# A hybrid encoder block on one core: S5 steps behind the gate copies, keys stacked before queries on another queue, a pool placed lower, and row pairs 64 bytes apart

## The chip, the cores and the metric

The kernel runs on one core of one Trainium2 chip. The metric is the device time of one execution in microseconds (us). The time before is the median of three timed runs, 1764.08 us (1761.85 to 1765.89). One more execution was taken with the hardware profiler; it took 1765.39 us, and its traced span is 1763.6 us.

## The reference, cut to what matters

One layer of an encoder block is applied to two request groups with the same weights: a prompt of 256 tokens and a sample of 512 tokens, 768 token rows in all, of width 1024. Everything is float32.

```python
def layer(x, mem, ...):
    h = rmsnorm(x, norm_mix_g)
    u, q, k, v, qm, gl = split(h @ w_in)              # 1024, 1024, 1024, 1024, 1024, 3072 columns
    z = gelu(s5(u, forward) + s5(u, backward) + d * u)  # 64 groups of 16 channels, 64 complex states
    s5_out = z * sigmoid(z @ s5_w_glu)
    diff_out = diff_attention(q, k, v)                # 8 heads, two softmax maps each, rotary, q/k norms
    mem_out = memory_attention(qm, rmsnorm(mem))      # 4 heads, 256 memory tokens
    br = stack([s5_out, diff_out, mem_out]) @ w_branch   # three 1024 x 1024 products
    merged = sum_n(sigmoid(gl_n + b_gate_n) * br_n)
    x = x + merged @ w_out
    g, up = split(rmsnorm(x) @ w_gate_up)
    return x + (silu(g) * up) @ w_down
```

## The kernel before, in words

**Products.** A float32 product is made of three TensorE products of rounded parts: each operand is split into a high part and a low remainder, and `mm3` (L748) issues high by high, high by low and low by high (L751 to L753). So each matrix of activations lies in SBUF as a pair of tiles: `H` (the normalised rows), `z`, `s5o` (the S5 branch's output), `xd` (differential attention's output), `mgd` (the merged rows), `f` and `dxh`/`dxl` (the FFN's). `pair(pool, name)` makes two tiles in a pool; `s5o` and `mgd` take the place that `H` had, on the right-hand side of SBUF. In nearly all products one operand is a pair of rows and the other a pair of weights, `wh` and `wl`. Names in the profile carry them: `wo<-wh,mgdhi` is a product of the output projection with the high parts of the merged rows.

**Weights.** `WStream` loads half of a weight chunk at a time (512 KB) on SyncE's queue, and splits it ahead of use: `wh` by a ScalarE copy (L595), `wl` by a VectorE subtraction (L601), or, while `by_dma` is set, by a ScalarE copy (L598) and a DMA that adds.

**Order.** The program is written as Python loops over chunks. Other work is woven in by generators that a "pace" advances by a tick per piece. A tile scheduler with a simulated timeline then fixes the order of the instructions on each engine; `tc.issue_after(x)` lets it place the following instructions only behind `x`. A tile's address follows from its pool: pools are stacked from two sides of SBUF, and a pool that is opened over the place of closed ones waits for those tiles' last users.

**The stages on TensorE.** (1) Memory keys, values and queries, and the cross attention, whose output becomes `Xm`. Within it and after it come the u chunks 0 to 3: eight 128-row tiles `ut`, each filled from two products (256 tokens copied by VectorE at L1075, 512 by ScalarE at L1073) and stored by SyncE to `u_scr` (`u_flush`, L282). Before a tile is filled, GpSimd zeroes three of its columns (L277). Chunks 0 and 1 use two buffers. Chunks 2 and 3 run while VectorE derives the S5 parameters, the last of which is `s5bb` (L242); their tiles come in turn from the pool `up` on the right and `up3` on the left. `up3` lies where the S5 work pool `pq` is opened afterwards, and the first tile of `pq` is `G`.

(2) The gates `gl`: 24 tiles of 128 columns, M = 0 to 23, in 12 weight chunks, each tile with a 256-token and a 512-token part that ScalarE copies out as `glt` (L1116). Between them the S5 steps run by ticks. For a group of four, `build` makes `G` on VectorE (L293, L296 to L298) and four small copies `s5bpad` on ScalarE (L310), and `response` multiplies them on TensorE (`psK`, L326). During M = 2 and 3 the ticks are bound behind the gate copy.

(3) Differential attention. Per head, `stack(h, i)` (L1217) transposes queries (i = 0) or keys (i = 1) on TensorE (`qkT`, L1230), makes the high parts on ScalarE (L1236) and the remainders on VectorE (`kl`, L1238; queries L1240); a head's keys are also copied to the other half of the partitions by two DMAs on GpSimd's queue (L1244, `kst<-kst`). The scores `sc` of the head (L1279, L1280) need all of it. In `diff_attend` head 0 is stacked queries first. `finish` (L1332) scales a head's output into `do`, and a DMA on ScalarE's queue stores that to `br_scr` (L1340).

(4) The branch of cross attention (`branch(2)`), woven with the tail of differential attention; at its last chunk `tail` closes attention's pools and opens the pool `XB`, in which the pair `z` is made (`zhi`, L745 on ScalarE, `zlo` on VectorE) for the half-GLU `glu`. `do` was the last tile of the pool `da2`, in the range over which `XB` is placed. Then come branch 0 with `s5o`, branch 1 with `xd`, whose last step writes the pair `mgd`, the output projection `wo` (512 columns of weights move against the rows of `mgd`), and the FFN with its products `gate`, `up` and `dn`.

Of the kernel before, what the change touches and what calls it, by code (L numbers as in the profile page):

```python
# [8 lines left out]
F32 = mybir.dt.float32  # L9
F32R = mybir.dt.float32r  # L10
# [13 lines left out]
class S5:  # L24
# [362 lines left out]
    def states(self, qd):  # L387
# [33 lines left out]

        S, T = new("X", 3), new("T", 1)
        i = slice(1, n - 1)
        vt(S[:, :, i], W[:, :, i], cs[:, i].unsqueeze(1).to_broadcast([128, 2, n - 2]), mul)
        vt(T[:, :, i], W[:, ::-1, i], sn[:, ::-1, i], mul)
        vt(S[:, :, i], S[:, :, i], T[:, :, i], add)
        S = [S[:, c].rearrange("p (g k) -> p g k", g=4)[:, :, 1:98] for c in range(2)]
        st["S"] = S

    def outputs(self, qd, y_scr):  # L430
# [3 lines left out]
        i = slice(1, 98)  # L434
        U, TT, S = st["U"], st["TT"], st["S"]
        G = st["G"]
# [50 lines left out]
TOK = 768  # L487
# [139 lines left out]
def hybrid_block(ctx, tc, A, outs, consts):  # L627
    nc = tc.nc
    v, act, gp, pe = nc.vector, nc.scalar, nc.gpsimd, nc.tensor
# [18 lines left out]
    def uid(s):  # L648
        cnt[0] += 1
        return f"{s}_{cnt[0]}"  # L650
# [167 lines left out]

    hctx, qctx, mctx = ExitStack(), ExitStack(), ExitStack()
    hp_ = hctx.enter_context(tc.tile_pool(name="H", bufs=1, side="right"))  # L820
    H = tuple(hp_.tile([128, 8, TOK], F32R, name=f"H{w}", tag="X" + w) for w in ("hi", "lo"))
    k1 = qctx.enter_context(tc.tile_pool(name="ma1", bufs=1, side="right"))
    mrs = k1.tile([128, 4], F32, name="mrs")
    k2 = qctx.enter_context(tc.tile_pool(name="ma2", bufs=2, side="right"))
# [48 lines left out]
    def mem_q(h):  # L873
# [9 lines left out]
        for sg, (c0, n) in enumerate(SEGS):  # L883
            sq = k3.tile([128, 2, n], F32, name=uid("mqsq"), tag=f"mqsq{sg}")
            sqs.append(sq)
            for m in range(2):
                ps = psd("mq")
                dense_fm(ps, w, m, H, c0, n)
                split_evac(qTh[:, m, c0 : c0 + n], qTl[:, m, c0 : c0 + n], ps[:, 0:n])
# [81 lines left out]
    with tc.tile_pool(name="nrm", bufs=1) as pool, tc.tile_pool(name="nrmg", bufs=1) as pg:  # L971
# [14 lines left out]
        for t0 in (0, 2):  # L986
            for k0 in range(0, 8, 2):
                ps = env.psb("nT")
                pv = ps.rearrange("p (k t) -> p k t", k=2)
                for k in range(2):  # L990
                    for t in range(2):
                        c = 128 * (k0 + k)
# [46 lines left out]
        for tt in range(TILES):  # L1039
            to_features(norm_rows(pool, xr[tt], rs[tt], g), H, tt)  # L1040
            next(units)
# [16 lines left out]
    s5 = S5(nc, tc, env, A, consts)  # L1058
    s5.open_dram(s5ctx)
    uctx = ExitStack()  # L1060
    up = uctx.enter_context(tc.tile_pool(name="utp", bufs=2))

    def u_chunk(c, tick, pools=None):
        w = W.get()
        for m in range(2):
            ut = s5.u_tile(pools[m] if pools else up, 2 * c + m)
            for sg, (c0, n) in enumerate(SEGS):
                ps = psd("u")
                dense_fm(ps, w, m, H, c0, n)
                src = ps[:, 0:n].rearrange("p (k j) -> p j k", j=8)  # L1070
                dst = ut[:, ::-1, 1:33] if sg == 0 else ut[:, ::-1, 34:98]
                if sg:
                    act.activation(dst, src, AF.Copy)  # L1073
                else:
                    v.tensor_copy(dst, src)  # L1075
                tick(1.0 + sg)
            s5.u_flush(ut, 2 * c + m)
# [12 lines left out]
    up = uctx.enter_context(tc.tile_pool(name="utp2", bufs=1, side="right"))  # L1090
    with tc.tile_pool(name="s5gap", bufs=1) as gap, tc.tile_pool(name="s5scr", bufs=1) as scr:

        gap.tile([128, 512], F32, name="s5gap")
        s5.params(scr, env.psb)
        with tc.tile_pool(name="utgap", bufs=1) as gap2, tc.tile_pool(name="utp3", bufs=1) as up3:
            gap2.tile([128, 9372], F32, name="utgap")
            for c in (2, 3):
                u_chunk(c, lambda w: None, (up, up3))
    uctx.close()


    with ExitStack() as c2:
        s5.open_work(c2)
        psum(1, b=4, w=1, d=2)
        glp = c2.enter_context(tc.tile_pool(name="glp", bufs=2))
        pace = Pace(s5.steps(y_scr), S5_RATE)
        for c in range(12):
            W.by_dma = True
            w = W.get()
            for m in range(2):  # L1110
                M = 2 * c + m
                for sg, (c0, n) in enumerate(SEGS):
                    gt = glp.tile([128, 512], F32, name=uid("glt"), tag="glt")
                    ps = psd("gl")
                    dense_fm(ps, w, m, H, c0, n)
                    out = act.activation(gt[:, 0:n], ps[:, 0:n], AF.Identity, bias=bg[:, M : M + 1])  # L1116
                    nc.sync.dma_start(gl_scr[M][:, c0 : c0 + n], gt[:, 0:n])
                    with tc.issue_after(out.ins) if M in (2, 3) else ExitStack():
                        pace.tick(1.0 + sg)
        pace.drain()  # L1120
    psum(2, a=2, b=3, d=3)
# [2 lines left out]

    x1ctx, xbctx, dctx, wctx = (ExitStack() for _ in range(4))
    stg = x1ctx.enter_context(tc.tile_pool(name="stg", bufs=2))
    k1 = dctx.enter_context(tc.tile_pool(name="da1", bufs=1))
    k2 = dctx.enter_context(tc.tile_pool(name="da2", bufs=2))
    q1 = wctx.enter_context(tc.tile_pool(name="dq1", bufs=1))
# [2 lines left out]
    tC = q1.tile([128, 4, 4, 64], F32, name="ropeC")  # L1132
    tS = q1.tile([128, 4, 4, 64], F32, name="ropeS")
    nlam = k1.tile([128, 1], F32, name="nlam")
    k2.tile([128, TOK], F32, name="do_", tag="do", bufs=1)

    rp = q1.tile([128, TILES, 256], F32, name="ropesrc", tag="ropet")
    tab, lv = (rp[:, t].rearrange("p (t c) -> p t c", c=64) for t in range(2))
# [31 lines left out]
    KL = [k1.tile([128, TOK], F32R, name=f"kl{i}") for i in range(4)]  # L1170
    for i, t in enumerate(KL):
        gp.memset(t[64 - 64 * (i % 2) : 128 - 64 * (i % 2)].bitcast(F32), 0.0)
    RO, VV, ST = {}, {}, {}

    def qk_units(h):
        w = W.get()
# [2 lines left out]
        for tt in range(TILES):  # L1179
            ps = psd("qk")  # L1180
            dense_tm(ps, w, 0, 256, H, tt)
            act.activation(r[:, tt], ps[:, 0:256], AF.Copy)
# [34 lines left out]
    def stack(h, i):  # L1217

        ro = RO[h]
        tag = "qk"[i]
        T = [k2.tile([128, TOK], F32R, name=uid(tag + "st"), tag=f"{tag}{m}") for m in range(2)]
        if i:
            kl = KL[2 * (h % 2) : 2 * (h % 2) + 2]
        for t0, t1 in ((0, 2), (2, 6)):
            ps = env.psb("qkT")
            for t in range(t0, t1):
                pe.transpose(ps[:, 128 * (t - t0) : 128 * (t - t0) + 128],  # L1230
                             ro[:, t, 128 * i : 128 * i + 128], env.ident)
            cs = slice(128 * t0, 128 * t1)
            for m in range(2):
                s, o = slice(64 * m, 64 * m + 64), slice(64 - 64 * m, 128 - 64 * m)
                src = ps[s, 0 : 128 * (t1 - t0)]
                act.activation(T[m][s, cs], src, AF.Copy)  # L1236
                if i:
                    v.tensor_tensor(out=kl[m][s, cs], in0=src, in1=T[m][s, cs].bitcast(F32), op=sub)  # L1238
                else:
                    v.tensor_tensor(out=T[m][o, cs], in0=src, in1=T[m][s, cs].bitcast(F32), op=sub)  # L1240
        if i:
            for m in range(2):
                s, o = slice(64 * m, 64 * m + 64), slice(64 - 64 * m, 128 - 64 * m)
                gp.dma_start(T[m][o], T[m][s])  # L1244
            ST[h] = ST[h] + [T, kl]
            RO.pop(h)
        else:
            ST[h] = [T]

    def diff_attend():  # L1250

        while 0 not in RO:
            yield
        stack(0, 0)
        yield
        stack(0, 1)
        for _ in range(2):
            yield
        N = 8 * TILES
        X = {}  # L1260
# [70 lines left out]

        def finish(h):  # L1332
            osb = X.pop(("h", h))[0]
            do = k2.tile([128, TOK], F32, name=uid("do"), tag="do", bufs=1)
            for t0, t1 in ((0, 2), (2, 6)):
                ps = env.psb("oT")
                for t in range(t0, t1):
                    pe.transpose(ps[:, 128 * (t - t0) : 128 * (t - t0) + 128], osb[:, t], env.ident)
                act.activation(do[:, 128 * t0 : 128 * t1], ps[:, 0 : 128 * (t1 - t0)], AF.Copy, scale=subg)
            act.dma_start(br_scr[h], do)  # L1340

        for i in range(N + 5):
            h, tt = divmod(i, TILES)
# [46 lines left out]
    with tc.tile_pool(name="gelu", bufs=1) as yp:  # L1390
        for m in range(2):
            gelu_load(m, yp)
        for j, h in enumerate(DIFF_HEADS):
# [3 lines left out]
            for n_v, u_ in enumerate(v_units(last // 2) if h is None else qk_units(h)):  # L1397
                n_unit += 1
                W.by_dma = n_unit >= LOADED and not final
                m, r = divmod(n_unit, GELU_UNITS)  # L1400
# [4 lines left out]
                if final and n_v % 2:  # L1405

                    t = slice(128 * (n_v - 1), 128 * (n_v + 1))
# [77 lines left out]
    with ExitStack() as c5:  # L1485
        c5.push(hctx)
        XA = hp_
# [5 lines left out]
        def pair(pool, nm):  # L1493
            return tuple(pool.tile([128, 8, TOK], F32R, name=uid(nm + w), tag="X" + w) for w in ("hi", "lo"))

        def branch(n_, X, first=False, MG=None, tick=None, hook=None):
            for c in range(4):
# [76 lines left out]

        branch(2, Xm, first=True, tick=dat.tick, hook=tail)
        x1, XB, Z = L["x1"], L["XB"], L["Z"]
        S = pair(XA, "s5o")
        for c in range(4):
            w = W.get()
            if c == 0:  # L1580
# [6 lines left out]
            for m in range(2):  # L1587
                M = 2 * c + m
                t = gtp.tile([128, TOK], F32, name=uid("gt"), tag="glr")
# [17 lines left out]
                    tc.keep_in_program_order(gp.dma_start(x1[t], xs[t]))  # L1607

        branch(0, S, hook=rows_in)
        MG = pair(XA, "mgd")  # L1610
        branch(1, Xd, MG=MG)
        mgctx.close()
        psum(3, d=5, b=3)
# [37 lines left out]
        for c in range(2):  # L1651
            w = [W.get(False)]
# [203 lines left out]
    with ExitStack() as c7:  # L1856
# [12 lines left out]
        for i, (p, g) in enumerate(ITEMS):  # L1869
# [10 lines left out]
            for t in range(3):  # L1880
                c = slice(128 * t, 128 * t + 128)
# [3 lines left out]
            if g == NG - 1:  # L1885
                r, f, op = HOME[p]
                for t in range(3):
                    o = x1[3 * r + t][:, 512 * f : 512 * f + 512]
# [51 lines left out]
```

## Time and profile before

| | before |
|---|---|
| timed runs, us | 1761.85, 1764.08, 1765.89 (median 1764.08) |
| profiled execution, us | 1765.39 |
| its traced span, us | 1763.6 |
| TensorE busy, us (share of the span) | 1740.1 (99%) |
| VectorE busy | 1267.4 (72%) |
| ScalarE busy | 889.0 (50%) |
| GpSimd busy | 276.0 (16%) |
| mean granted TensorE clock | 0.997 |

TensorE's matmuls are pipelined: a duration of one is longer than the distance from its start to the next one's, so durations are compared with each other and not added. The number in brackets behind a row of the timeline is the idle time of the engine just before it, and what ended it. In the rows of windows the columns are the stretch, its length, the busy time of TensorE, its weight loads, VectorE, ScalarE and GpSimd (with the number of instructions), the granted TensorE clock, the DMA engines' busy share and GB/s.

### The profile page before, as it was taken

What the parts mean: (1) busy time and instruction counts of PE and PEld (TensorE: products, weight loads), DVE (VectorE), ACT (ScalarE), POOL (GpSimd) and SP (SyncE); (2) the same over time, 40 slices, a digit from 0 to 9 for tenths busy, and PEclk for the clock granted to TensorE, in tenths of its full rate; (3) what the DMA queues carried; (4) which work ended last, traced back from release to release, by engine and by line L of the source; (5) the groups of instructions that cost most, each with busy time, mean ns of one, the idle gap of its engine ahead of it and who ended that gap; (6) DMA issues with size and microseconds to landing.
All of it is one profiled execution on the core that took longest, in us unless ns stands there. A gap on an engine that the chain in (4) does not pass through costs nothing.

```text
span 1763.6 us, 29524 instructions
## 1 busy us (share of the span) xinstructions
PE 1740.1 (99%) x11242; PEld 1611.4 (91%) x11242; DVE 1267.4 (72%) x2349; ACT 889.0 (50%) x1856; POOL 276.0 (16%) x296
## 2 busy tenths in 40 slices
PE   9999999999999998999999999999999999999999
PEld 8999988899999998999989888888889999998887
DVE  6755747799999779797877535453598777776775
ACT  6444543786767347777765433232343333334443
POOL 0000000000000101101110002000026555551220
PEclk9999999999999999999999999999999999999999
DMA  7222635755556457345484337331322323238964
GB/s 252 83 90 88 129 118 116 183 130 150 142 158 158 123 137 193 80 107 118 104 196 129 122 115 247 124 104 59 90 76 99 108 90 108 90 108 272 265 142 109
DMA packets 209662, 234.11 MB, mean 133 GB/s; under 512 B 57832, under 2 KB 173296, under 8 KB 209520
## 3 DMA queue, kind: packets, MB, share of 16 engines
q1 hardware_dynamic: 184080, 164.05, 30.8%
q0 software_dynamic: 24288, 65.02, 17.3%
q10 hardware_dynamic: 1152, 3.15, 0.5%
q8 instruction: 89, 1.46, 0.3%
q14 instruction: 53, 0.43, 0.1%
HBM read 165.78 MB, written 41.22 MB: 117 GB/s over the span
## 4 chain that ended last, share of the span: by engine, by line
PE 59%; DMA 2%; issue 1%; DVE 1%; ACT 1%; POOL 0%; SPq 0%; DVEq 0%; ACTq 0%; POOLq 0%
PE br L752 4%; PE br L751 4%; PE br L753 4%; PE gate L751 3%; PE up L751 3%; PE gate L753 3%; PE up L752 3%; PE gate L752 3%; PE up L753 3%; PE dn L752 3%; PE dn L753 3%; PE dn L751 3%; PE av L1316 2%; PE qk L752 2%; PE qk L753 2%; PE qk L751 2%
## 5 line engine op out<-in xcount | busy, mean ns | idle before, releaser
L595 ACT ACTIVATE wh<-wr 128x1024 fp32r<-128x1024 f32 x124 | 140.6, 1134 | 69.1 <-PE br L752 28.3
L601 DVE TENSOR_TENSOR wl<-wr,wh 128x1024 fp32r<-128x1024 f32 x82 | 108.4, 1325 | 83.8 <-ACT wh L595 81.9
L751 PE MATMUL gl<-Hhi,wh 128*128 128x256 f32 (+1 forms) x384 | 132.0, 344 | 0.0
L753 PE MATMUL gl<-Hhi,wl 128*128 128x256 f32 (+1 forms) x384 | 129.1, 336 | 0.0
L752 PE MATMUL gl<-Hlo,wh 128*128 128x256 f32 (+1 forms) x384 | 129.0, 336 | 0.0
L751 PE MATMUL qk<-wh,Hhi 128*128 128x256 f32 x384 | 108.8, 283 | 1.1 <-ACT V L1214 0.7
L752 PE MATMUL qk<-wl,Hhi 128*128 128x256 f32 x384 | 109.1, 284 | 0.0
L599 POOL DMA_DIRECT2D wl<-wr x42 | 36.6, 872 | 459.4 <-ACT wl L598 442.5
L753 PE MATMUL qk<-wh,Hlo 128*128 128x256 f32 x384 | 108.3, 282 | 0.0
L752 PE MATMUL dn<-wld,dxh 128*128 128x512 f32 x231 | 89.6, 389 | 0.0
L751 PE MATMUL dn<-whd,dxh 128*128 128x512 f32 x231 | 89.5, 389 | 0.0
L753 PE MATMUL dn<-whd,dxl 128*128 128x512 f32 x231 | 88.9, 389 | 0.0
L753 PEld LDWEIGHTS gl<-Hhi,wl 128*128 128x128 f32 x384 | 72.2, 188 | 7.9
L752 PEld LDWEIGHTS gl<-Hlo,wh 128*128 128x128 f32 x384 | 72.4, 189 | 7.3
L751 PEld LDWEIGHTS gl<-Hhi,wh 128*128 128x128 f32 x384 | 72.4, 189 | 6.9
L751 PEld LDWEIGHTS qk<-wh,Hhi 128*128 128x128 f32 x384 | 73.1, 190 | 2.2 <-ACT V L1214 0.9
L557 ACT ACTIVATE wh_S<-ws 128x512 fp32r<-128x512 f32 x70 | 41.2, 626 | 65.5 <-PE up L752 35.2
L752 PEld LDWEIGHTS qk<-wl,Hhi 128*128 128x128 f32 x384 | 73.1, 190 | 0.6
L753 PEld LDWEIGHTS qk<-wh,Hlo 128*128 128x128 f32 x384 | 73.3, 191 | 0.3
L1285 DVE TENSOR_REDUCE nm<-sc 128x1 f32<-128x512 f32 (+1 forms) x96 | 56.9, 599 | 22.2 <-PE sc L1280 21.3
L1287 ACT ACTIVATE p<-sc,nm 128x512 f32<-128x512 f32 (+1 forms) x96 | 59.1, 618 | 22.4 <-DVE nm L1285 22.1
L558 DVE TENSOR_TENSOR wl_S<-ws,wh_S 128x512 fp32r<-128x512 f32 x70 | 58.0, 852 | 16.2 <-ACT wh_S L557 16.2
(481 smaller groups left out, 6025.0 us busy)
## 6 DMA issues: line engine op xcount, KB each, us to landing
wr<-in_w_in_dram SPq DMA_DIRECT2D x48, 512.0 KB, 5.0
wr<-in_w_gate_up_dram SPq DMA_DIRECT2D x44, 512.0 KB, 3.6
wl<-wr POOLq DMA_DIRECT2D x42, 512.0 KB, 5.2
wr<-in_w_branch_dram SPq DMA_DIRECT2D x24, 512.0 KB, 4.3
glr<-gl_scr POOLq DMA_DIRECT2D x24, 384.0 KB, 3.4
hid_scr<-fa SPq DMA_DIRECT2D x11, 768.0 KB, 6.4
wr<-in_w_mem_kv_dram SPq DMA_DIRECT2D x16, 512.0 KB, 3.5
wr<-in_w_in_dram SPq DMA_DIRECT2D x32, 256.0 KB, 4.4
```

The lines of the kernel that those rows point to most:

```text
L557: self.nc.scalar.activation(f(hi), src, AF.Copy)
L558: self.nc.vector.tensor_tensor(out=f(lo), in0=src, in1=f(hi).bitcast(F32), op=ALU.subtract)
L595: self.nc.scalar.activation(hi, r, AF.Copy)
L599: self.nc.gpsimd.dma_start(lo, r.bitcast(F32R), accum_op=ALU.add)
L601: self.sub.tensor_tensor(out=lo, in0=r, in1=hi.bitcast(F32), op=ALU.subtract)
L751: pe.matmul(ps, wh, xh, start=start, stop=False, **kw)
L752: pe.matmul(ps, wh, xl, start=False, stop=False, **kw)
L753: pe.matmul(ps, wl, xh, start=False, stop=stop, **kw)
L1285: v.tensor_reduce(out=nm[:, m : m + 1], in_=ps, axis=AX.X, op=ALU.max, negate=True)
L1287: act.activation(pm[:, 0:n], ps, AF.Exp, bias=nm[:, m : m + 1], accum_out=s1s[:, tt : tt + 1] if m == 0 else s2)
L1316: pe.matmul(po[:, 0:128], aT[:, 128 * k : 128 * k + 128], V[:, c0 // 128 + k, 128 * (h % 2) : 128 * (h % 2) + 128], start=(k == 0), stop=( ...
```

## The change: what it does

The change has five parts.

1. `u`: chunks 2 and 3 use one tile (`up`, one buffer, on the right); the second pool `up3` and the filler below it are gone. Each `ut` of these chunks is zeroed after the tile before it has been stored.
2. Gates: the ticks of the S5 steps are bound behind the gate copies for M = 0 to 3, and not only for M = 2 and 3.
3. `do` gets a pool of its own, `dop`, opened below attention's pools, in a range that `XB` does not cover.
4. Head 0 is stacked keys first. The copies of the keys go out on SyncE's queue for heads 0 and 7, and stay on GpSimd's for the others. `ST[h]`, which the scores wait for in the program, is filled when both halves are there.
5. `rows_pair` makes `H`, `s5o` and `mgd`: tiles that are 64 bytes longer, with the high part at the start and the low part 64 bytes in, or, for `mgd`, the other way round. In the addresses as built, taken modulo 256 bytes, the weights `wh` and `wl` are at 160 before and after. `H` and `s5o` were at 224 and 224 (high, low) and are at 96 and 224; `mgd` was at 224 and 224 and is at 160 and 160. `z`, `xd`, `f` and the `dn` operands are at 160 in both.

```diff
-    H = tuple(hp_.tile([128, 8, TOK], F32R, name=f"H{w}", tag="X" + w) for w in ("hi", "lo"))
+    def rows_pair(nm, off=0):
+        ts = (hp_.tile([128, 8 * TOK + 16], F32R, name=nm + w, tag="X" + w) for w in ("hi", "lo"))
+        return tuple(t[:, o : o + 8 * TOK].rearrange("p (k t) -> p k t", k=8) for t, o in zip(ts, (off, 16 - off)))
+
+    H = rows_pair("H")
...
-            ut = s5.u_tile(pools[m] if pools else up, 2 * c + m)
+            ut = s5.u_tile(up, 2 * c + m)
...
-        with tc.tile_pool(name="utgap", bufs=1) as gap2, tc.tile_pool(name="utp3", bufs=1) as up3:
-            gap2.tile([128, 9372], F32, name="utgap")
-            for c in (2, 3):
-                u_chunk(c, lambda w: None, (up, up3))
+        u_chunk(2, lambda w: None)
+        u_chunk(3, lambda w: None)
...
-                    with tc.issue_after(out.ins) if M in (2, 3) else ExitStack():
+                    with tc.issue_after(out.ins) if M < 4 else ExitStack():
...
+    dop = dctx.enter_context(tc.tile_pool(name="dop", bufs=1))
     k1 = dctx.enter_context(tc.tile_pool(name="da1", bufs=1))
     k2 = dctx.enter_context(tc.tile_pool(name="da2", bufs=2))
...
-    k2.tile([128, TOK], F32, name="do_", tag="do", bufs=1)
...
-                gp.dma_start(T[m][o], T[m][s])
-            ST[h] = ST[h] + [T, kl]
+                (nc.sync if h in (0, 7) else gp).dma_start(T[m][o].bitcast(F32), T[m][s].bitcast(F32))
+            half[h, 1] = [T, kl]
+        else:
+            half[h, 0] = [T]
+        if (h, 1 - i) in half:
+            ST[h] = half.pop((h, 0)) + half.pop((h, 1))
             RO.pop(h)
-        else:
-            ST[h] = [T]
...
+        stack(0, 1)
+        yield
         stack(0, 0)
-        yield
-        stack(0, 1)
...
-            do = k2.tile([128, TOK], F32, name=uid("do"), tag="do", bufs=1)
+            do = dop.tile([128, TOK], F32, name=uid("do"), tag="do")
...
-        S = pair(XA, "s5o")
+        S = rows_pair("s5o")
...
-        MG = pair(XA, "mgd")
+        MG = rows_pair("mgd", 16)
```

What stands on ScalarE from the last `u` copies to the first gate copies, before (`s5bpad` are the copies that `psK` waits for, `wh` and `wl` splits of weights, `ut` copies of u, `glt` copies of gates):

```order
L1073 ACTIVATE ut_3616<-u_3646 128x8x64
L310 ACTIVATE s5bpad_3463<-s5bb 64x4x16 x2
L595 ACTIVATE wh_0_3753<-wr_0_3488 128x1024
L598 ACTIVATE wl_0_3754<-wr_0_3488 128x1024
L310 ACTIVATE s5bpad_3465<-s5bb 64x4x16 x2
L595 ACTIVATE wh_1_3760<-wr_1_3608 128x1024
L1073 ACTIVATE ut_3673<-u_3703 128x8x64
L598 ACTIVATE wl_1_3761<-wr_1_3608 128x1024
L1116 ACTIVATE glt_3767<-gl_3768,bg 128x256
L1116 ACTIVATE glt_3795<-gl_3796,bg 128x512
```

And after, at the same place:

```order
L1077 ACTIVATE ut_3609<-u_3639 128x8x64
L595 ACTIVATE wh_0_3744<-wr_0_3481 128x1024
L598 ACTIVATE wl_0_3745<-wr_0_3481 128x1024
L595 ACTIVATE wh_1_3751<-wr_1_3601 128x1024
L1077 ACTIVATE ut_3666<-u_3696 128x8x64
L598 ACTIVATE wl_1_3752<-wr_1_3601 128x1024
L1118 ACTIVATE glt_3758<-gl_3759,bg 128x256
L1118 ACTIVATE glt_3786<-gl_3787,bg 128x512
L310 ACTIVATE s5bpad_3463<-s5bb 64x4x16 x2
L310 ACTIVATE s5bpad_3465<-s5bb 64x4x16 x2
```

The four `s5bpad` copies have moved from ahead of the last `u` copy to behind both gate copies of M = 0. On TensorE `psK` moves six products up and stands right behind the 512-token part of M = 1.

SyncE's queue around head 0's stacking, before (`z_scr` are stores of S5's output, `y` loads of it, both of stage 2's tail):

```order
L1385 DMA z_scr_135<-zz_8304 16x8x768
L450 DMA y_8467<-y_scr_129 128x8x97
L1385 DMA z_scr_136<-zz_8615 16x8x768
L450 DMA y_8843<-y_scr_130 128x8x97
L1385 DMA z_scr_137<-zz_9032 16x8x768
L450 DMA y_9211<-y_scr_131 128x8x97
```

And after:

```order
L1389 DMA z_scr_135<-zz_8297 16x8x768
L450 DMA y_8460<-y_scr_129 128x8x97
L1389 DMA z_scr_136<-zz_8608 16x8x768
L1246 DMA kst_7813<-kst_7813 64x768
L450 DMA y_8836<-y_scr_130 128x8x97
L1246 DMA kst_7814<-kst_7814 64x768
L1389 DMA z_scr_137<-zz_9025 16x8x768
L450 DMA y_9204<-y_scr_131 128x8x97
```

The two copies of head 0's keys stand around one `y` load, behind the store of `z_scr_136`.

ScalarE at the end of attention, before (`do` is the last head's output, `brr` the rows of `z` as loaded):

```order
L595 ACTIVATE wh_0_12468<-wr_0_12183 128x1024
L1339 ACTIVATE do_12119<-oT_12120,subg 128x256
L1339 ACTIVATE do_12119<-oT_12124,subg 128x512
L1340 DMA br_scr_182<-do_12119 128x768
L595 ACTIVATE wh_1_12474<-wr_1_12348 128x1024
L745 ACTIVATE zhi_12309<-brr_12311 128x768
L745 ACTIVATE zhi_12309<-brr_12315 128x768
```

And after:

```order
L595 ACTIVATE wh_0_12462<-wr_0_12176 128x1024
L1343 ACTIVATE do_12112<-oT_12113,subg 128x256
L1343 ACTIVATE do_12112<-oT_12117,subg 128x512
L745 ACTIVATE zhi_12303<-brr_12305 128x768
L745 ACTIVATE zhi_12303<-brr_12309 128x768
L745 ACTIVATE zhi_12303<-brr_12313 128x768
L745 ACTIVATE zhi_12303<-brr_12317 128x768
L745 ACTIVATE zhi_12303<-brr_12321 128x768
L1344 DMA br_scr_182<-do_12112 128x768
L595 ACTIVATE wh_1_12468<-wr_1_12342 128x1024
```

Five splits of `z` have moved ahead of the store of `do` and of the split of the next weights.

More of the change, by code (lines that the diff above doesn't have):

```diff
@@ L1061, in hybrid_block, with u_chunk @@
     up = uctx.enter_context(tc.tile_pool(name="utp", bufs=2))
-    def u_chunk(c, tick, pools=None):
+    def u_chunk(c, tick):
         w = W.get()
         for m in range(2):
-            ut = s5.u_tile(pools[m] if pools else up, 2 * c + m)
+            ut = s5.u_tile(up, 2 * c + m)
             for sg, (c0, n) in enumerate(SEGS):
@@ L1172, in hybrid_block @@
         gp.memset(t[64 - 64 * (i % 2) : 128 - 64 * (i % 2)].bitcast(F32), 0.0)
-    RO, VV, ST = {}, {}, {}
+    RO, VV, ST, half = {}, {}, {}, {}
     def qk_units(h):
```

## The prediction

> **What bounds the kernel now.** I read the page's busy times first, then TensorE's list of waits, and then the windows around the two longest of them.
>
> The page, its head and the shares of the chain that ended last:
>
> ```profile
> span 1763.6 us, 29524 instructions
> ...
> PE 1740.1 (99%) x11242; PEld 1611.4 (91%) x11242; DVE 1267.4 (72%) x2349; ACT 889.0 (50%) x1856; POOL 276.0 (16%) x296
> ```
>
> TensorE is busy for 1740.1 of 1763.6 us. A change can therefore shorten the kernel in three ways only: by an idle time of TensorE that goes, by products that follow each other faster, or by a clock that stays up. Its waits, as what was waited for, the sum, how often, and the longest:
>
> ```profile
> PE sc L1279 <- DMA kst<-kst: 4.3, 2, 2.8
> PE psK L326 <- DMA wr<-in_w_in_dram: 2.8, 1, 2.8
> PE glu L751 <- ACT zhi L745: 2.2, 1, 2.2
> ```
>
> These three are the longest, and the change touches each of them. The windows before and after the two of 2.8 us (TensorE's busy time, weight loads, VectorE, ScalarE, GpSimd, then the granted clock):
>
> ```profile
> 313.40:316.84 3.44, 0.61 (x5) 0.56 (x5) 3.40 (x5) 1.49 (x2) 0.86 (x1) 1.00 1.07 325
> 316.84:320.26 3.42, 3.42 (x17) 3.42 (x18) 3.38 (x6) 1.86 (x3) 0.86 (x1) 0.50 0.65 163
> 675.24:678.66 3.42, 0.60 (x5) 0.39 (x4) 3.21 (x7) 2.21 (x5) 0.00 (x0) 1.00 1.24 265
> 678.66:682.07 3.41, 3.41 (x17) 3.41 (x18) 3.38 (x9) 2.14 (x7) 0.58 (x1) 0.50 0.83 257
> ```
>
> Both times TensorE worked for about 0.6 of some 3.4 us, and both times the next 3.4 us ran at half clock, which loses half of them, 1.7 us. So each of these waits costs 2.8 us and another 1.7 us behind it.
>
> **Part by part.** All sums go against the profiled execution, 1765.39 us (span 1763.6). The median of the timed runs, 1764.08, is 1.3 us below it.
>
> *u and gates.* The rows of the timeline around `psK`:
>
> ```profile
> 298.08 1.23 DVE L242 TENSOR_TENSOR s5bb<-s5bb,csc 128x1024 f32<-128x1024 f32 x1
> 304.56 0.69 ACT L1116 ACTIVATE glt<-gl,bg 128x512 f32<-128x512 f32 x1 [1.76 <-PE gl L753]
> 308.35 1.23 DVE L293 TENSOR_TENSOR G<-s5C,s5Ar 128x1024 f32<-128x1024 f32 x1 [9.04 <-DMA u_scr<-ut]
> 315.37 1.27 DVE L298 TENSOR_TENSOR G<-G,ptG 128x512 f32<-128x512 f32 x2
> 316.25 0.46 PE L326 MATMUL psK<-G,s5bpad 128*128 128x128 f32 x2 [2.83 <-DMA wr<-in_w_in_dram]
> ```
>
> The wait is put down to a load of weights, but the row before it shows the true one: the last add of `G` ran from 315.37. VectorE had finished `s5bb` at 299.3 and stood for 9.04 us, because `G` lies where the last `ut` did and that was being stored. With the tile on the right `G` has no such wait. It starts when `s5bb` is done, at 300.4 to 301.3 (allowing 1 to 2 us for the stall below and the last copy of u), and what lies between its first instruction and its last add took 315.37 + 1.27 - 308.35 = 8.3 us, so it is ready by about 309.6. TensorE reached `psK` at 316.25 - 2.83 = 313.4, later still with the stall below. The other operand is now late by order: the `s5bpad` copies stand behind the 512-token gate copy of M = 0, which ends at 304.56 + 0.69 = 305.3 and slips with the stall to 306.5. Four small copies, each no longer than that gate copy, add at most 2.8: 309.3. Both are 4 us early. Gain: **-2.83**, and the half-clock stretch behind it.
>
> What this adds is a wait inside chunk 3. One tile now serves all four, so each waits for the store of the one before it:
>
> ```profile
> 275.17 0.37 SPq L282 DMA_DIRECT2D u_scr<-ut  x1
> ...
> 279.53 0.15 POOL L277 MEMSET ut<- 128x8 f32 x2 [8.41 <-DMA u_scr<-ut]
> ...
> 283.70 0.45 SPq L282 DMA_DIRECT2D u_scr<-ut  x1
> ...
> 286.27 0.42 DVE L1075 COPY ut<-u 128x256 f32<-128x256 f32 x1
> ...
> 290.65 0.39 PE L751 MATMUL u<-Hhi,wh 128*128 128x512 f32 x1
> ...
> 291.20 0.18 POOL L277 MEMSET ut<- 128x8 f32 x3 [11.48 <-DMA u_scr<-ut]
> ```
>
> The store of `ut5` is issued at 283.70 and what waits for it goes on at 291.20. Before, `ut6` was in the other pool and VectorE could copy its 256-token part when it was there (the 286.27 row is that copy's slot). After, the zeroing of `ut6` starts at 291.2, and the copy of 0.42 us ends near 291.9. TensorE's product at 290.65 needs the PSUM bank which that copy empties, so it stands for 1.25 us. The other end: `ut4`'s store took 279.53 - 275.17 = 4.4 us, and as short a one would land at 288.1 and leave 0.1. A longer one than 7.5 us has no row, and I put 1.5 as the upper end. I take **+1.25**, since it is this store's own time. Behind the waiting VectorE copy stand the S5 parameters, which the 9.04 us cover. On SyncE's queue the weight loads keep their places around these stores.
>
> *Head 0's keys.* The chain that ended last and the timeline there:
>
> ```profile
> 673.67 4.76 DMA kst<-kst
> ```
>
> ```profile
> 664.34 0.53 SPq L1385 DMA_DIRECT2D z_scr<-zz  x1
> ...
> 666.58 0.59 ACT L1236 ACTIVATE qst<-qkT 64x512 fp32r<-64x512 f32 x1
> ...
> 672.49 0.43 DVE L1238 TENSOR_TENSOR kl<-qkT,kst 64x256 fp32r<-64x256 f32 x1
> ...
> 678.48 0.44 PE L1279 MATMUL sc<-kst,qst 128*128 128x256 f32 x1 [2.82 <-DMA kst<-kst]
> ```
>
> The second copy of the keys is issued when ScalarE has made their high part, at 673.67, and takes 4.76 us, while TensorE stands from 675.66. After, keys and queries change places: the keys' last high part is the one at 666.58, done at 667.2, and its DMA lands 4.76 later, at 672.0. On SyncE's queue it stands behind the store at 664.34, which has left by then, and it delays one `y` load by about its issue of 0.5 us; that load feeds S5's output, for which no row of the waits of TensorE stands. The queries now come in the late place, but they need no DMA: their remainder on VectorE takes the slot of 672.49, and the last, 512-token one the slot after it, both before 675.66. Gain: **-2.82**, and its half-clock stretch. Head 7's copies change queue too, but no wait of `sc` belongs to it; 0.
>
> *Clock.* Two stretches of 3.41 us at half speed, 1.7 us each: **-3.4** if they go with their idle times. The Trainium skill, page "TensorE: Matmul & The Clock Gate", section "What's actually happening", says that the clock falls after at least one idle window of about 3.4 us; these idle times are 2.8 us, and by the letter of it they would not be the cause. That makes a rival of its own below.
>
> *The z pair.* The chain at the end of attention, and the first product of the half-GLU in the timeline:
>
> ```profile
> 998.81 1.05 ACT do L1339 x2
> ...
> 999.88 2.73 DMA br_scr<-do
> ...
> 1002.71 0.85 ACT zhi L745
> ```
>
> ```profile
> 1003.61 0.39 PE L751 MATMUL glu<-zhi,wh 128*128 128x256 f32 x1 [2.15 <-ACT zhi L745]
> ```
>
> `zhi` is held by the DMA that stores `do`, since `XB` lies over `do`. With `do` in `dop` the first `zhi` runs at 999.86, right behind `do`, and is done at 1000.7; TensorE comes at 1001.46. Its remainder on VectorE takes about as long again, until 1001.6, and is wanted after four products, near 1002.4. Gain: **-2.15** (at least 1.85, if the remainder slips by a few tenths). The store of `do` and the split of the next half of weights go behind five `zhi` of 0.85 us, to about 1004.1; that half is wanted only at the fifth of eight steps of the product, each of which takes TensorE some 2 us, and `do` is read back only for `xd`, behind all of `glu`.
>
> *Merged rows.* The products of the output projection and those of `dn`, which have the same form (512 columns of weights move, rows stand):
>
> ```profile
> L751 PE MATMUL dn<-whd,dxh 128*128 128x512 f32 x231 | 89.5, 389 | 0.0
> L753 PE MATMUL dn<-whd,dxl 128*128 128x512 f32 x231 | 88.9, 389 | 0.0
> ...
> L753 PE MATMUL wo<-wh,mgdlo 128*128 128x512 f32 x96 | 37.8, 395 | 0.0
> L752 PE MATMUL wo<-wl,mgdhi 128*128 128x512 f32 x96 | 37.8, 395 | 0.0
> L751 PE MATMUL wo<-wh,mgdhi 128*128 128x512 f32 x96 | 37.8, 397 | 0.0
> ```
>
> `dn`'s rows have the weights' residue modulo 256 bytes, 160; `mgd` did not and now does. 96 x (8 + 6 + 6) ns = **-1.9**, if the address is what divides them. Against that: the Trainium skill, page "SBUF — State Buffer", section "Who interferes with whom", gives TensorE two independent read ports, one for the moving operand and one for weight loads. By it the residue is worth nothing, and the sum is 1.9 higher; nothing but these rows speaks for a price here.
>
> *H and s5o.* Their low part keeps its residue, 224, and their high part goes from 224 to 96; neither had the weights' residue and neither gets it. How much a residue can be worth in 256-wide products is seen here (`z` at 160, `s5o` and H at 224):
>
> ```profile
> L752 PE MATMUL qk<-wl,Hhi 128*128 128x256 f32 x384 | 109.1, 284 | 0.0
> ...
> L753 PE MATMUL v<-wh,Hlo 128*128 128x256 f32 x192 | 53.8, 280 | 0.0
> ...
> L753 PE MATMUL glu<-zhi,wl 128*128 128x256 f32 x64 | 18.1, 283 | 0.0
> ...
> L751 PE MATMUL br<-s5ohi,wh 128*128 128x256 f32 x64 | 17.9, 279 | 0.0
> ```
>
> The rows differ by about 4 ns whether or not the residues agree, and `qk` and `v` differ by 4 with the same `H`. I take **0**. In the listing by form, 5232 products have `H` or `s5o` as an operand; 1296 are 512 wide, where `dn` against `wo` spans 389 to 397. A gain of 3 ns on those 1296 would be 3.9 us, and 3.6 ns more on all 5232 would be 18.8.
>
> Sum: -2.83 + 1.25 - 2.82 - 3.4 - 2.15 - 1.9 = -11.85, so 1765.39 - 11.85 = **1753.5 us**. Against the median it would be 1752.2.
>
> **The rivals.**
>
> *The half-clock stretches stay.* They might belong to something else at those places. For it: 2.8 us of idling is short of a whole stretch of 3.4 us. (The rule of the Trainium skill cited above asks for a whole window.) Against it: they are the two stretches right behind the two longest idle times, to the microsecond. 1753.5 + 3.4 = 1756.9.
>
> *The residue of `mgd` is worth nothing.* `wo` could be slower for its own reason, such as its adds. For it: `glu`, with the weights' residue, is no faster than `s5o` without it, 283 against 279 ns. (So is the port rule of the Trainium skill cited above.) Against it: the products of `wo` have no wait in the list. 1753.5 + 1.9 = 1755.4.
>
> *H's move costs a little.* Apart by 128 bytes, high and low parts may take 1 to 1.5 ns more in each of 5232 products: +5 to +8, so 1758.7 to 1761.4. For it: 4 ns lie between rows of one form; against it: neither residue meets the weights'.
>
> *H's move costs much (the other side).* Here the same 5232 products pay more than 2.3 ns each, which eats up all of 11.85; at 3.6 ns it is 1753.5 + 18.8 = 1772.3. It decides for slower from (11.85 + 3.5) / 5232 = 2.9 ns. For it: 4 ns between rows is more than that. Against it: it would have to be all of them.
>
> *The waits come back.* The change may not free `psK` and `sc`, because something else is as late: `G` behind other VectorE work, the keys behind SyncE's stores. Then only the z pair and `mgd` gain, and the stall stays: 1765.39 - 2.15 - 1.9 + 1.25 = 1762.6. Against it: 4 us of room at both places.
>
> **How the numbers follow.** Forecast 0.52; half clock stays 0.10; `mgd` worth nothing 0.10; H costs a little 0.11; waits come back 0.09; H costs much 0.08. A measurement of this kernel tells about 0.2% (3.5 us) from no change, as the three runs before lie 4 us apart; so faster means below 1760.6, slower above 1767.6. Forecast, half clock, `mgd` and most of the mild case (0.08) make 0.80; the rest of the mild case and the waits, 0.12; the heavy one 0.08. The range starts at 1748.5, which is the forecast with H's gain of 3.9 and a little of the distance to the median. It ends at 1761.5, behind the mild case; the waits and the heavy case, 0.17, lie above.
>
> **What would show it.** In the changed profile: no wait of `psK`, `glu` or head 0's `sc`; clock 1.00 in the stretches after 316 and 678; a wait of some 1.2 us of the last `u` tile; `wo` at 389 to 390; `gl`, `qk`, `v` within 1 ns. I am wrong if `qk` or `gl` move by more than 2 ns, if a half-clock stretch stands where no idle time does, or if `psK` waits for `s5bpad`.

## The result and the profile after

The change makes the kernel faster by 5.1 us, where 10.5 against the median had been forecast (1753.5 in all): 1758.9 us (median of 21 runs, 1756.73 to 1761.49) against 1763.99 before (21 runs, 1760.16 to 1766.76), ratio 0.9975 with a 95% interval of 0.9968 to 0.9982. The profiled execution took 1759.81 us, 5.6 less than the one before. The time lies between the ends that the prediction gave, but the gain is less than half of what it forecast.

The page after, head and busy times:

```profile
span 1758.0 us, 29514 instructions
...
PE 1741.6 (99%) x11242; PEld 1613.5 (92%) x11242; DVE 1266.8 (72%) x2349; ACT 887.1 (50%) x1856; POOL 274.5 (16%) x292
```

The span is 5.6 us shorter and TensorE is busy for 1.5 us more. So 7.1 us of idle time went, and 1.5 us came back as work, though the two stretches at half clock that had made TensorE's work longer are gone (a new one stands at 921 us, so that this profile has one fewer in all). TensorE's list of waits after:

```profile
PE sc L1283 <- ACT p L1291: 2.0, 3, 1.4
PE sc L1283 <- DMA kst<-kst: 1.4, 1, 1.4
...
PE qkT L1232 <- DVE kl L1240: 1.3, 1, 1.3
PE qk L751 <- ACT qksq L1186: 1.2, 1, 1.2
...
PE u L751 <- DVE ut L1079: 0.2, 1, 0.2
```

`psK` and `glu` are gone from it. Head 0's wait for its keys is gone too (the one of 1.4 that is left is head 6's). But `qk` now waits for ScalarE's `qksq` near that place and `sc` for ScalarE's `p`, and the wait of `qkT`, 1.7 before, is 1.3. The stall of `u` is 0.2 us and not 1.25. Around `psK` the windows (TensorE, its weight loads, VectorE, ScalarE, GpSimd, granted clock) now read:

```profile
313.40:316.84 3.44, 3.44 (x25) 3.14 (x25) 2.28 (x4) 3.11 (x4) 0.45 (x1) 1.00 0.80 278
316.84:320.26 3.42, 3.42 (x28) 3.29 (x27) 0.20 (x1) 2.52 (x5) 0.83 (x2) 1.00 0.82 159
```

TensorE is busy throughout at full clock. `G` starts when `s5bb` is done and not 9 us later:

```profile
299.76 1.23 DVE L242 TENSOR_TENSOR s5bb<-s5bb,csc 128x1024 f32<-128x1024 f32 x1
301.02 1.23 DVE L293 TENSOR_TENSOR G<-s5C,s5Ar 128x1024 f32<-128x1024 f32 x1
```

The output projection's products, by form, are at `dn`'s 389 ns now, or within 2 ns of it:

```profile
L753 PE MATMUL wo<-wh,mgdlo 128*128 128x512 f32 x96 | 37.2, 389 | 0.0
L751 PE MATMUL wo<-wh,mgdhi 128*128 128x512 f32 x96 | 37.2, 391 | 0.0
L752 PE MATMUL wo<-wl,mgdhi 128*128 128x512 f32 x96 | 37.2, 389 | 0.0
```

Where the gain went is seen in a stretch in which TensorE never idles, 690 to 900 us (mostly `qk` and `v`). Before:

```profile
690.00:900.00 210.00, 210.00 (x1740) 1.00 0.55 121
```

And after:

```profile
690.00:900.00 210.00, 210.00 (x1730) 1.00 0.56 123
```

In the same 210 us at the same clock TensorE got 10 products fewer done, 1.2 us of work. The mean durations don't tell this, since matmuls overlap: `qk<-wl,Hhi` reads 284 ns in both. The distance from a product's start to the next one's start does. As means over all products of a group (gaps of over 1.25 times the median left out), before and after: `qk` 116.2 and 117.3 ns, `v` 114.8 and 117.1, `gl` of 512 columns 229.3 and 231.3, `mk` 115.6 and 117.8, `wo` 233.4 and 226.9. Times the number of products: `H` and `s5o` cost +5.9 us, the memory rows +0.6 (their place lies under `H`'s pool and went from 224 to 96 with it), `wo` gives -1.9.

### The profile page after: what moved, and what is told of

Read it like the earlier page. It is cut to its first block, busy times and chain, and to the rows that moved or that the text cites. A ratio compares the mean times of both kernels' runs of the same rounds, so it can differ in the third digit from the quotient of the medians.

```text
span 1758.0 us, 29514 instructions
## 1 busy us (share of the span) xinstructions
PE 1741.6 (99%) x11242; PEld 1613.5 (92%) x11242; DVE 1266.8 (72%) x2349; ACT 887.1 (50%) x1856; POOL 274.5 (16%) x292
## 4 chain that ended last, share of the span: by engine, by line
PE 59%; DVE 2%; DMA 1%; issue 1%; ACT 1%; POOL 0%; SPq 0%; ACTq 0%; DVEq 0%; POOLq 0%
PE br L753 4%; PE br L751 4%; PE br L752 4%; PE gate L751 3%; PE gate L753 3%; PE up L753 3%; PE gate L752 3%; PE up L752 3%; PE up L751 3%; PE dn L753 3%; PE dn L751 3%; PE dn L752 3%; PE av L1320 2%; PE qk L752 2%; PE qk L753 2%; PE qk L751 2%
```

## The experiments

They were timed in three groups, each beside runs of the kernel before: the addresses back, the addresses alone and both runs on the keys (before: median 1764.17); the sweeps, u and gates undone and the better version (1763.73); the other three (1764.1). Each median is of 5 to 12 runs, but the sweeps have one run each. Where the text compares with the change, that is its 1758.9, from a group of its own, and differences from it of about 1 us are not clear of the noise.

**Addresses back.** H and s5o at 224 again, mgd at 160.

```diff
-        ts = (hp_.tile([128, 8 * TOK + 16], ...) for w in ("hi", "lo"))
-        return tuple(t[:, o : o + 8 * TOK]... for t, o in zip(ts, (off, 16 - off)))
+        t = hp_.tile([128, 16 * TOK + 16], F32R, name=nm, tag="X")
+        return tuple(t[:, o : o + 8 * TOK]... for o in (off, off + 8 * TOK))   # off: H, s5o 16; mgd 0
```

> The changed kernel with H and s5o at residue 224 for both parts again, mgd kept at 160 (one tile with 64 bytes of room for both parts; the memory rows end up at 160). Theory A (the move of H's high part to 96 took back what the waits gave): gl, u, mq and br of 512 columns return from about 232 ns per product to 229, qk and v from 117 to 115, 5 to 6 us in all, so 1753 us. Theory B (the address of H costs nothing, the missing gain was lost to new waits alone): 1758.9, within 0.7.

1756.95 us (ratio to before 0.9961, 0.9948 to 0.9973), 2.0 faster than the change: between the two. The trace says why not more: `qk`, `v`, `gl` and the others of H are back at the distances of before (116.0, 114.8, 229.3 ns, 5.9 us in all), but the memory rows at 160 made `mk` and `mv` slower, 119.6 ns each, 2.1 us. That leaves 3.8 us, of which 2.0 are seen. Some of the rest stands in waits that are longer than in the change, now that the products ahead of them are faster: those for ScalarE's `V` by 0.8 us, the stall of `u` by 0.5.

**Addresses alone.** The kernel before with `rows_pair` for H, s5o and mgd; nothing else.

> The kernel before with only the row pairs changed (H and s5o at 96 and 224, mgd at 160 and 160), every order of instructions as before. Theory A: H, s5o and the memory rows cost 5.5 to 6.5 us, mgd gives 1.9: 4 to 4.6 us slower than before, 1768. The prediction's step (H nothing, mgd 1.9): 1762.1.

1766.3 us (1.0014, 1.0005 to 1.0023), 2.1 slower than before. The sign of theory A, half its size. The distances sum to +4.5 us as expected; `psK`'s wait shrank from 2.8 to 2.3 us, so part of the slower work in front of it was hidden in a wait that stood there anyway. Alone, the fifth part of the change is a loss.

**Everything but the addresses.** The change with plain tiles, all rows at 224; the order of instructions is the change's.

```diff
-        ts = (hp_.tile([128, 8 * TOK + 16], ...) ...
+        return tuple(hp_.tile([128, 8, TOK], F32R, name=nm + w, tag="X" + w) for w in ("hi", "lo"))
```

> The changed kernel without its fifth part: H, s5o, mgd and the memory rows at 224 as before, the order of all instructions as in the change. Theory A (by the spacing of the products, the residues cost 6.4 us at H, s5o and the memory rows, 1.0 to 1.5 of it hidden in waits, and give 1.9 at mgd): 3 to 3.5 us faster than the change, 1755.5. Theory B (the residues cost nothing): 1.9 slower than the change for mgd, 1760.8.

1755.55 us (0.9956, 0.9944 to 0.9968): theory A. The same stretch as above, in this kernel:

```profile
690.00:900.00 210.00, 210.00 (x1738) 1.00 0.59 130
```

The first four parts together are worth 8.5 us; the fifth took 3.4 of it back.

**mgd alone.** The kernel before with mgd at 160, the rest at 224 (the one-tile form above, and 192 bytes more below the memory rows).

> The kernel before with mgd alone moved, to 160; H, s5o and the memory rows stay at 224. The prediction's step: 1.9 us faster than before, 1762. If the residue is worth nothing: 1763.9.

1762.54 us (0.9989, 0.998 to 0.9997), 1.6 faster; the prediction's 1.9 lies within its interval, which just leaves out zero. The distances of `wo` show the gain more clearly: 226.8 ns against 233.4.

**Two sweeps of residues** (one run each).

```diff
+        t = hp_.tile([128, 16 * TOK + 48], F32R, name=nm, tag="X")   # high, low at any residue from 32 to 224
```

> The changed kernel with other residues only: H at 32 and 192 (high, low), s5o at 64 and 128, memory rows at 32, mgd at 160. If the distance to the weights' 160 decides: 192 and 128 (32 bytes off) dearest, 32 (128 off) cheapest in 512-wide products. If only 160 itself is special: all near 229 ns per 512-wide product.

> The changed kernel with other residues only: H at 64 and 128, s5o at 96 and 160, memory rows at 32, mgd at 160. If the residue alone sets the pace, s5o's high part at 96 reads 232 ns per 512-wide product as in the changed kernel and its low part at 160 reads 227 to 229 as z and xd do; H's two parts then show 64 and 128.

1764.37 and 1768.4 us, 5.5 and 9.5 us above the change. The stretch from 690 to 900 us in the first sweep:

```profile
690.00:900.00 210.00, 210.00 (x1716) 1.00 0.54 121
```

And in the second:

```profile
690.00:900.00 210.00, 210.00 (x1704) 1.00 0.51 118
```

Distances in ns from a product's start to the next one's, by the residue of the rows, weights at 160 (the row of 160 from products of `z` and `xd`, where rows and weights agree, and from `mv` in the first experiment; 96 from the change, 224 from before, the others from the sweeps):

| residue of the rows | 512 columns moving (`gl`) | 256 columns, rows stationary (`v`) |
|---|---|---|
| 160 | 227 to 230 | 120 |
| 224 | 228 to 230 | 115 |
| 32 | 230 to 233 | 118 to 119 |
| 192 | 231 | 118 |
| 96 | 232 to 233 | 116 to 118 |
| 128 | 233 | 120 |
| 64 | 233 to 235 | 119 to 120 |

The distance to the weights' residue does not decide: 32 is farthest from 160 and not the cheapest, 192 and 128 are equally near and differ in the 512-wide ones. Nor is 160 alone special. Nor does a product's own residue say all: in the second sweep s5o's low part at 160 read 234.9 and not 227 to 229, behind a high part at 96, and in the change `v` with H's low part went from 114.7 to 116.6 though that part stayed at 224. So more than a product's own residue counts. The operands of the neighbouring products may be it; no run tests them alone. Why the address matters at all stays open.

**Keys undone.** The change with head 0 queries first and all key copies on GpSimd's queue.

> The changed kernel with head 0 stacked queries first again and all key copies on GpSimd's queue. The prediction's step (the keys' wait of 2.8 us and a half-clock stretch of 1.7 us behind it): 4.5 us slower than the change, 1763.4. Theory A (the wait was mostly replaced by waits for ScalarE and VectorE, only about 0.6 us and part of a half-clock stretch were gained): 1 to 2 us slower, 1760 to 1761. Nothing gained: 1758.9.

1759.76 us (0.9973, 0.9964 to 0.9982), 0.9 slower than the change. That is not the prediction's 4.5; but the two intervals overlap, so theory A and no gain at all can't be told apart by the time. In its trace head 0's wait for the keys is back, 3.5 us, and the waits of `qk` for `qksq` and of 1.4 us for `p` are gone.

**Keys first, on GpSimd's queue.**

> The changed kernel with head 0's key copies on GpSimd's queue, keys still first. If the copies on SyncE's queue hold up the load of y, and through it ScalarE and the two new waits of TensorE (qk 1.2 us, sc 1.4 us): these shrink by about 1 us in all, 1758. If VectorE and ScalarE are simply full there: the same waits, 1758.9 within 0.4.

1759.11 us (0.9969, 0.9957 to 0.9981): no difference in the time. Of the three waits two are the same (`p` 1.4, `kl` 1.2 us), and the queue isn't their cause. The third is not: `qk` waits for `qksq` for 0.3 us instead of 1.2. (In the eight profiles with keys first and these copies on SyncE's queue it is 0.7 to 1.7.) ScalarE's row of the `y` load, in the change and then in this run, points to the reason:

```profile
670.11 0.85 ACT L1381 ACTIVATE yt<-y 128x776 f32<-128x776 f32 x1 [2.18 <-DMA y<-y_scr]
```

```profile
668.22 0.85 ACT L1381 ACTIVATE yt<-y 128x776 f32<-128x776 f32 x1 [1.05 <-DMA y<-y_scr]
```

With the copies on SyncE's queue ScalarE stands 1.1 us longer for `y`, and the copies of the queries and of `qksq` come behind that in its order. In the time the 0.9 us don't show: they are within the noise, and the profile has other waits that are longer by 0.2 to 0.3. The windows of the change show what else stands there (TensorE, weight loads, VectorE, ScalarE; the first window is around the wait for `qksq`, the second around that for `p`):

```profile
671.20:674.70 3.50, 2.32 (x21) 2.11 (x19) 3.36 (x5) 3.40 (x7) 0.00 (x0) 1.00 0.55 151
678.66:682.07 3.41, 1.97 (x17) 1.90 (x17) 3.36 (x14) 2.31 (x7) 0.57 (x1) 1.00 0.80 226
```

VectorE is busy for 3.36 us of both windows, and ScalarE for 3.40 of the first. They also carry S5's output (`yt`, `zz`) there. That they caught up before, while TensorE stood for the keys, fits the run with the keys undone, but no run shows it by itself.

**u and gates undone.** Two pools for u, ticks bound only for M = 2 and 3.

> The changed kernel with the u tiles and the gates' ticks as before. The prediction's steps: psK's wait of 2.8 us and 1.7 us of half clock return, the stall of 1.25 goes: 3.3 us slower than the change, 1762.2. With the stall of only 0.2 that the trace after shows: 1763.2. If the half-clock stretch doesn't belong to the wait: 1761.5.

1761.1 us (ratio to before 0.9982, 0.9972 to 0.9992), 2.2 slower than the change, nearest to the last of the three numbers. `psK` waited for 2.2 us and not 2.8, since the slower products in front of it hid 0.6; and in its profile no stretch at half clock followed (over its 12 runs the clock was 0.9990 on average, against 0.9992 in the change). These are the two windows that the prediction shows of the kernel before; the wait, from 315.53 to 317.74, lies across both here:

```profile
313.40:316.84 3.44, 2.13 (x13) 1.67 (x11) 3.44 (x4) 3.21 (x4) 0.86 (x1) 1.00 1.02 359
316.84:320.26 3.42, 2.52 (x21) 2.48 (x22) 3.39 (x7) 1.74 (x3) 0.00 (x0) 1.00 0.94 202
```

**do undone.** `do` in attention's pool.

> The changed kernel with do in attention's pool again, as before. The prediction's step: the wait of the z pair returns, 2.1 to 2.2 us slower than the change, 1761.1. Against it: other waits near the end of attention shrink for it, 1759.5.

1762.49 us (0.9991, 0.9982 to 0.9999), 3.6 slower than the change, more than expected. The wait is back with 2.1 us, and in this profile it is followed by a stretch at half clock, which it was not before (mean clock of its 11 runs 0.9984):

```profile
999.60:1003.00 3.40, 1.27 (x6) 0.79 (x5) 2.34 (x3) 2.36 (x3) 0.00 (x0) 1.00 0.85 270
1003.00:1006.41 3.41, 3.41 (x12) 2.77 (x12) 3.41 (x5) 2.48 (x4) 1.61 (x3) 0.50 0.74 237
```

**A better version.** The change with H, s5o and the memory rows at 224, mgd at 160, and head 6's key copies on SyncE's queue too.

```diff
+        t = hp_.tile([128, 16 * TOK + 16], F32R, name=nm, tag="X")   # as in the first experiment
-    k0.tile([128, 48], F32, name="gap")
+    k0.tile([128, 96], F32, name="gap")                          # memory rows 192 bytes lower: 224
-                (nc.sync if h in (0, 7) else gp).dma_start(...)
+                (nc.sync if h in (0, 6, 7) else gp).dma_start(...)
```

> The changed kernel with H, s5o and the memory rows at 224 again, mgd at 160, and head 6's key copies on SyncE's queue as well. Theory A: against the residue run before (1757.0), the memory rows give back the 2.1 us that 160 cost them, plus 0.6 that 96 costs, and head 6's wait of 1.4 us goes: 1753. Theory B (addresses are worth no more than the 2 us seen, and a wait that goes there is replaced by another, as at head 0): 1756.5.

1751.18 us (0.9932, 0.992 to 0.9944), 12.5 us faster than before and 7.7 faster than the change (5 runs), better than theory A. Head 6's wait of 1.4 us for its keys is gone and nothing stands in its place; `mk` is at 114.8 ns. Its list of waits begins:

```profile
PE sc L1283 <- ACT p L1291: 2.0, 3, 1.4
PE qkT L1232 <- DVE kl L1240: 1.6, 1, 1.6
```

And the same 210 us:

```profile
690.00:900.00 210.00, 210.00 (x1739) 1.00 0.59 131
```

## Why the prediction was wrong, point by point

- **H and s5o: "I take 0".** This is the step that failed. By the distances it measured +5.9 us, and with the memory rows, which no step had named, +6.5. The two kernels without this loss (1755.55, and 1751.18 with the gain of `mgd` and head 6's copies) show that it is the addresses. The reason given, that neither residue meets the weights', rested on rows with the residues 160 and 224; none of them was at 96. The rows did differ by 4 ns within one form, and I read that as noise about zero rather than as the size of what an address can do. Nor would the sign named in advance, a move of `qk` or `gl` by more than 2 ns, have shown it in the durations: the rows of `qk` and `gl` moved by 2 ns at most, those of `qk` downwards. The count was wrong too: the 5232 products are 4464 with H or s5o and 768 with the memory rows. The rival "H's move costs a little", 1 to 1.5 ns in each of the 5232 and 1758.7 to 1761.4 us, had a chance of 0.11 and is what came: 6.5 us / 5232 = 1.2 ns, 1758.9 us. That its total agrees too is partly luck, since the 2.2 us that the keys didn't bring are about what the stall that stayed away (1.0) and shorter waits for `V` (1.0) gave.
- **Head 0's keys: -2.82.** Over-sized. The keys came in time as worked out (no wait for them is left), but "what is late next" was answered for the keys and queries alone. The banks of `qk` and `sc` are emptied by ScalarE and VectorE, and these were no earlier than before: head 0's waits went from 2.82 + 1.70 to 1.29 + 1.18 + 1.44 us, a gain of 0.6. Undoing the part cost 0.9, within the noise. The step had also let the later `y` load pass, since no wait of TensorE stood for it; by the run on GpSimd's queue 0.9 of the 1.18 us go with it, and the other two waits stand without it.
- **u and gates: -2.83, stall +1.25.** Right for `psK`. The stall was 0.18, and not because the store was faster: it was issued at 284.88 and GpSimd went on at 291.95, 7.1 us later, against the 7.5 worked out from before:

```profile
284.88 0.45 SPq L282 DMA_DIRECT2D u_scr<-ut  x1
...
291.95 0.15 POOL L277 MEMSET ut<- 128x8 f32 x2 [11.07 <-DMA u_scr<-ut]
```

  TensorE came later, and the slower products before it are at least part of that: in the six kernels that have them and the single tile the stall is 0.2 to 0.8 us, in the three with the rows at 224 it is 0.7 to 1.1 (0.9 in the better version).
- **The z pair: -2.15.** Right, as the list of waits shows; undoing it cost more, 3.6, and the next point has the likely reason.
- **Clock: -3.4.** Right in size, but not as a stretch that belongs to a place. Every run has its mean granted clock. The runs of before beside the first experiments took 1763.3 us on average at 0.998 (10 runs), 1764.8 at 0.997 (9) and 1766.2 at 0.996 (3), so 0.001 is about 1.4 us. Over the 23 runs of before in that group the clock was 0.9972, over the 21 of the change 0.9992; 0.0020 of 1764 us is 3.5 us, and by the 1.4 it is 2.8. But which stretch is lost changes: the profile of the change has one at 921 us, behind some short waits, where before had none:

```profile
917.60:921.00 3.40, 2.08 (x8) 0.80 (x6) 3.18 (x10) 3.30 (x11) 0.00 (x0) 1.00 0.00 0
921.00:924.42 3.42, 3.32 (x13) 3.15 (x14) 3.29 (x10) 2.38 (x8) 1.50 (x3) 0.51 0.06 16
```

  Head 6's wait for its keys is 12 us earlier and isn't the cause: the better version, without that wait, has the same stretch at 913.64.

  The wait of 2.1 us led to such a stretch with `do` undone, one of 2.2 us at `psK` did not, nor did one of 2.9 in the run with mgd alone. Where the wait falls fits all of these. In each profile the half-clock stretches begin whole steps of 3.413 us apart: before at 13.06, 316.84 and 678.66 us, 89 and 106 steps. Both waits of 2.8 us lay whole in one step (TensorE busy for 0.61 and 0.60 us in the prediction's windows). In the run with u and gates undone they begin at 13.03 and 678.63, 195 steps apart. A step ends at 316.8 there, which cuts the wait of 2.2 us and leaves TensorE busy for 2.13 and 2.52 us of the two steps. The wait of 2.9 is cut likewise (1.84 and 2.13). The wait of `glu` was cut before (2.15 us; 1.94 and 2.69 busy) and lay whole in a step with `do` undone (2.1 us; 1.27). So the two stretches that the prediction counted are those of one execution, and another can cut the same waits elsewhere. The Trainium skill, page "TensorE: Matmul & The Clock Gate", section "What's actually happening", has the window free-running, which these runs fit; its idle window of about 3.4 us is not needed: TensorE was busy for 1.27 and for 2.08 of 3.4 us ahead of two of them.
- **Merged rows: -1.9.** Right: -1.9 by the distances, 1.6 in time. The Trainium skill's rule of independent ports (page "SBUF — State Buffer", section "Who interferes with whom") would have made it nothing, as it would the loss at H; here the measurements decide against it.

The terms as they came, in us: -2.8 (`psK`) +0.2 (u) -0.6 (keys) -3.5 (clock) -2.2 (z) -1.9 (mgd) +6.5 (H, s5o and the memory rows) = -4.3, against -5.1 measured. Of the difference, 1.0 us is found in waits of `qk` and `v` for ScalarE's `V`, 1.3 before and 0.3 after, in which slower products hid.

## What to carry to other kernels

When a change moves a large operand, cost the new address of every product that reads it, and of what lies below it, with the distance between product starts and not with their durations; one part's small loss per product, times thousands, ate most of what three removed waits had brought. When a wait goes, ask which engines its consumer needs next: if they are busy for nearly all of the window, or stand in order behind a load that the change delays, a wait comes back under another name. A part of a change that is right for one operand (here the merged rows) can be kept alone.

## What the runs showed of the hardware

The pace of TensorE's products depends on the SBUF addresses of rows and weights modulo 256 bytes, by up to 4% (227 to 235 ns at 512 columns, 115 to 120 at 256), at full clock and without any wait, and on more than a product's own residue.

Half-clock stretches of 3.41 us begin on a grid of 3.413 us that holds through one execution. In the 13 profiles, after the first 5 us, each step with TensorE busy for less than 1.5 us was followed by half clock; no stretch began behind a step with more than 2.3; in between both happened (2.08 with, 1.94 without), and what decides there stays open. So the same wait, 2.1 us for instance, costs a stretch when it lies whole in one step and none when a step's end cuts it.
